# Re-ordering the passages of a feed-forward block and summing seven products in one PSUM bank

## The chip, the cores and the metric
The kernel runs on one core of a Trainium2 chip. The metric is the device time of one execution in microseconds (us). Its engines are TensorE (PE in the profile; PEld is its weight load), VectorE (DVE), ScalarE (ACT), GpSimd (POOL) and SyncE (SP), which here only issues DMAs.

## The reference
One layer of a streaming encoder on 16 meta tokens + 1024 prompt frames + 32 sample frames (T = 1072 tokens) of width 1024: RMSNorm, a combined projection for a convolution group and a windowed attention group, an output projection with residual, and then the part that the change touches:
```
def conv_ffn(x, gate_past, g, w_up, dw_w, dw_b, w_down):
    h = rmsnorm(x, g)
    u = h @ w_up                                  # 1024 -> 2 x 2816
    gate, up = u[..., :D_FF], u[..., D_FF:]
    gate_ext = jnp.concatenate([gate_past, gate], axis=1)
    y = jax.nn.silu(depthwise_causal_conv(gate_ext, dw_w, dw_b)) * up     # width 3
    return x + y @ w_down, gate_ext[:, -(FFN_CONV_WIDTH - 1):]
...
y_prompt = rmsnorm(xp, norm_final)[:, N_META:]
```
All data are float32. A float32 product is made of three matmuls in a faster float32 form: each operand is split into a high and a low part (hi, lo), and hi x hi, hi x lo and lo x hi are summed.

## The kernel before
Channels lie on the 128 partitions, tokens along the free axis. Tokens are cut into three blocks (OB and YB: 324 or 320, 384 and 352 columns) for the norms and the down-projection, and into two row blocks p = 0, 1 of 2 x 266 and 2 x 264 columns for the up-projection.

**Order.** Inside the regions of manual_schedule the instructions of TensorE run in the order in which the program writes them; in the last region (the end of the down-projection) those of ScalarE and VectorE too. Everything else, the DMA issues of SyncE among them, is put in order by the planner of the tile framework, which knows dependencies and tile releases. Each engine then runs its own list in that order.

**The second norm.** rms2(2, ...) is a generator with three steps (rms_steps, L246 to 264): sums of squares by six tiny matmuls (L252) followed by a few tiny operations on VectorE, POOL and VectorE (L253 to 257); three diagonal matrices on ScalarE (L260); six matmuls that spread the result over the partitions, R (L263), and a copy to rbg. The squares come from ScalarE and are added on POOL (L271) in conv_half before it.

**The up-projection.** There are NF = 22 feed-forward tiles f. f = 0 and 1 are plain (group: 24 matmuls of 266 or 264 columns). Meanwhile t_stage (L1216 ff.: hraw, traw, th, tl) prepares operands for the rest: f = 2 to 21 run as a seven-product scheme (Strassen's, in Winograd's form) in which seven half-size products per p take the place of eight. product makes 12 matmuls (L1205), evac reads the bank out after each product into the gate row G (two halves) and the value row Y (two halves). gate_done normalises the gate, convolves it over three taps and applies SiLU; y_done multiplies and stores y to memory (yd). w_forms prepares the seven weights of the next f, a step after every second product.

**The down-projection.** The 22 y tiles are loaded back (y_load), split, and kept in the space of operands that are no longer needed (yrow). They are consumed in three chunks; in each, eight output tiles m are made for the blocks 1, 2 and 0. d_load loads and splits a weight. In the last chunk the final norm of a block runs beside the next block's matmuls.

Of the kernel before, what the change touches and what calls it, by code (L numbers as in the profile page):

```python
# [10 lines left out]
F32 = mybir.dt.float32  # L11
F32R = mybir.dt.float32r
AF = mybir.ActivationFunctionType
ALU = mybir.AluOpType
# [3 lines left out]
P = 128  # L18
D = 1024
KD = D // P  # L20
# [74 lines left out]
CHUNKS = ((0, 6), (6, 14), (14, 22))  # L95
# [62 lines left out]
def body(nc, tc, cp, wp, xp, dp, io):  # L158
# [961 lines left out]
    with tc.tile_pool(name="psB", bufs=1, space=PSUM, reuse_waits="tile") as pf:  # L1120
# [5 lines left out]
        u2s = [xf[0][:, GOW + T:GOW + T + PNS[0]], xf[2][:, GXW + GOW:GXW + GOW + PNS[1]]]  # L1126
# [73 lines left out]
        def product(ps, q, p, f, first, last):  # L1200
# [69 lines left out]
        def evac(f, p, what, ps):  # L1270
            G, _, Y = rows_of(f)
            n, a0 = PNS[p], PAT[p]
            b0 = a0 + n
            ya, yb, u2 = Y[:, a0:a0 + n], Y[:, b0:b0 + n], u2s[p]
            add = nc.vector.tensor_tensor
            if what == 1:
                nc.scalar.copy(ya, ps)
            elif what == 6:
                add(out=u2, in0=ya, in1=ps, op=ALU.add)
            elif what == 2:  # L1280
                nc.scalar.copy(G[:, g_at(a0):g_at(a0) + n], ps)
            elif what == 7:
                add(out=yb, in0=ya, in1=ps, op=ALU.add)
            elif what == 5:
                add(out=yb, in0=yb, in1=ps, op=ALU.add)
            elif what == 4:
                add(out=ya, in0=ya, in1=ps, op=ALU.add)
            else:
                for lo_, hi_, o in g_pieces(b0, n):
                    add(out=G[:, o:o + hi_ - lo_], in0=u2[:, lo_:hi_], in1=ps[:, lo_:hi_], op=ALU.add)  # L1290

        BANK = {1: 0, 2: 0, 6: 1, 7: 1, 4: 1, 5: 2, 3: 2}
        FIRST, LAST = (1, 6, 5), (2, 4, 3)
        SEQ_ = (1, 6, 2, 7, 5, 4, 3)

        def up_strassen(f, steps):
            gate_start(f)
            banks = {}
            for q, p in steps:
                k = p, BANK[q]  # L1300
                if q in FIRST:
                    banks[k] = mmt()[:, :PNS[p]]
                product(banks[k], q, p, f, q in FIRST, q in LAST)
                evac(f, p, q, banks[k])
                yield
            gate_done(f)
            y_done(f)
# [24 lines left out]
        for i in range(4):  # L1332
            group(0, 0, i // 2, i % 2)
            next(last_rms, None)
            next(t0s)
        gate_done(0)
# [27 lines left out]
        for f in range(2, NF):  # L1364
            steps = [(q, p) for q in SEQ_ for p in range(2)]
            forms = w_forms(f + 1) if f + 1 < NF else None
            for i, _ in enumerate(up_strassen(f, steps)):
                if forms and i % 2:
                    next(forms, None)
            for _ in forms or ():  # L1370
                pass

# [8 lines left out]
        trow = [trow[i] for i in (1, 4, 2, 5, 0, 3)]  # L1381
        sr = rows(sl, 4)
        yrow = trow + list(zip(rows(BH, KD), rows(BL, KD))) + trow + [(sr[0], sr[1]), (sr[2], sr[3])]
        stage = [xf[1][:, 0:ny], xf[1][:, ny:2 * ny], gx0[:, 0:ny], rbt[:, 0:ny]]

        def y_load(f):
            raw = stage[f % 2 + 2 * (f >= CHUNKS[0][1])]
            nc.sync.dma_start(raw, yd[f][:, NMETA:T])
            hilo(*yrow[f], raw)

        bhf, blf = flat(BH), flat(BL)
        dring = [plain[:2], plain[2:]]
        big = [(z[:, i * 1024:i * 1024 + 1024], w[:, i * 1024:i * 1024 + 1024]) for i in range(6)
               for z, w in ((bhf, blf),)]
# [8 lines left out]
        def d_load(ci, m):  # L1403
            f0, f1 = CHUNKS[ci]
            w = (f1 - f0) * P
            if ci == 2 and m > 1:
                hi, lo = big[m - 2]
            else:
                hi, lo = dring[dn[0] % 2]
                dn[0] += 1  # L1410
# [14 lines left out]

        for f in range(CHUNKS[0][1]):
            y_load(f)
        wn = [d_load(0, 0)]
        order = [(ci, m) for ci in range(3) for m in range(KD)]
        for i, (ci, m) in enumerate(order[:2 * KD]):  # L1430
            w = wn.pop(0)
            wn.append(d_load(*order[i + 1]))
            for b in (1, 2, 0):
# [14 lines left out]
            if ci == 0 and m == 7:  # L1448
                y_load(20)
                y_load(21)  # L1450
# [20 lines left out]
        wz = wp.tile([P, 1024], F32, tag="raw", name="raw")  # L1471
        scrs = [z[:, i:i + 384] for z in (rbg, gx0, wz) for i in (0, 384)]
# [120 lines left out]
```

## Time and profile before
| what | value |
|---|---|
| median of 3 runs (lowest to highest) | 1106.85 us (1106.69 to 1107.34) |
| profiled execution | 1108.38 us, of which the span from the first to the last instruction is 1106.4 us |
| mean granted clock of TensorE | 0.985 of full |
| busy: TensorE, VectorE, ScalarE, POOL | 97%, 72%, 40%, 13% |

A row of a timeline begins with start and duration in us, then engine, line, operation, output<-inputs, shape and count; a bracket at its end is the idle time before it and what ended it. The up-projection begins at 353 us, the seven-product phases at about 409, the down-projection at 821, its last chunk at about 1000.

### The profile page before, as it was taken

The page shows a single profiled execution, that of the slowest core. Times are in us where ns is not written, and L with a number is a line of the kernel's source. Part 1 is how long each engine was busy: PE and PEld are TensorE (multiplying, and loading weights), DVE is VectorE, ACT ScalarE, POOL GpSimd, SP SyncE. Part 2 cuts the span into 40 slices and gives each one's busy share as a digit, 9 for nine tenths or more (in the row PEclk, how much of TensorE's full clock was granted, in tenths as well). Part 3 has the DMA queues.
Part 4 walks back from the last instruction along what each step waited for, and adds up shares of the span by engine and source line. Part 5 has one row for each costly group of instructions (what it writes and reads, how often), then busy time and mean ns, then how long its engine had stood idle before and what let it go on. Part 6 is the DMA issues. An engine that isn't in the chain of part 4 may idle for free.

```text
span 1106.4 us, 18738 instructions
## 1 busy us (share of the span) xinstructions
PE 1068.1 (97%) x7547; PEld 1039.4 (94%) x7547; DVE 799.4 (72%) x1401; ACT 437.5 (40%) x890; POOL 142.0 (13%) x189
## 2 busy tenths in 40 slices
PE   8999999989998999999999999999989999999996
PEld 7989997759998999999999999999979999999996
DVE  7789999999787888788788788788784233223233
ACT  8521227995866752233233233232244331012111
POOL 1112000013334120000000000000001210001221
PEclk9999999999999899999999999999998999999998
DMA  7344331135843111312212212212268782112012
GB/s 260 79 105 101 83 92 39 39 67 83 158 138 129 39 59 67 108 59 75 100 59 78 97 58 78 97 59 79 99 200 231 151 186 67 40 39 86 11 57 100
DMA packets 45822, 103.75 MB, mean 94 GB/s; under 512 B 7840, under 2 KB 25496, under 8 KB 45736
## 3 DMA queue, kind: packets, MB, share of 16 engines
q1 hardware_dynamic: 35912, 84.46, 23.3%
q0 software_dynamic: 9536, 17.89, 9.7%
q8 instruction: 59, 0.97, 0.4%
q14 instruction: 27, 0.22, 0.1%
q10 hardware_dynamic: 288, 0.22, 0.1%
HBM read 72.41 MB, written 21.02 MB: 84 GB/s over the span
## 4 chain that ended last, share of the span: by engine, by line
PE 83%; DVE 6%; ACT 5%; DMA 4%; issue 2%; SPq 0%; POOLq 0%; POOL 0%; DVEq 0%; ACTq 0%
PE mm L1205 36%; PE mm L240 14%; PE mm L241 14%; PE mm L242 14%; DVE acc L357 2%; DMA x<-yd 1%; DMA raw<-wdn 1%; ACT pb L688 1%; DVE tl L1137 1%; PE R L263 1%; DMA xs<-xT 1%; ACT hraw L1225 1%; ACT th L1136 1%; DVE pb L681 1%; ACT glu L750 1%
## 5 line engine op out<-in xcount | busy, mean ns | idle before, releaser
L357 DVE SCALAR_TENSOR_TENSOR acc<-glu,prm,acc 128x1090 f32<-128x1090 f32 (+3 forms) x180 | 167.9, 966 | 0.4
L1205 PE MATMUL mm<-bh,sl 128*128 128x266 f32 (+1 forms) x544 | 117.8, 285 | 0.0
L240 PE MATMUL mm<-hi,whi 128*128 128x352 f32 (+3 forms) x312 | 105.2, 337 | 2.1 <-ACT hi L274 2.1
L241 PE MATMUL mm<-lo,whi 128*128 128x352 f32 (+3 forms) x312 | 102.4, 328 | 0.5 <-DVE lo L275 0.5
L242 PE MATMUL mm<-hi,wlo 128*128 128x352 f32 (+3 forms) x312 | 102.1, 327 | 0.0
L240 PE MATMUL mm<-bh,whi 128*128 128x320 f32 (+4 forms) x320 | 99.8, 312 | 0.0
L242 PE MATMUL mm<-bh,wlo 128*128 128x320 f32 (+4 forms) x320 | 99.4, 311 | 0.0
L241 PE MATMUL mm<-bl,whi 128*128 128x320 f32 (+4 forms) x320 | 99.4, 311 | 0.0
L1205 PEld LDWEIGHTS mm<-bh,sl 128*128 128x128 f32 x544 | 90.8, 189 | 0.0
L1205 PE MATMUL mm<-th,sl 128*128 128x264 f32 (+1 forms) x384 | 90.8, 285 | 0.0
L1205 PE MATMUL mm<-bl,sl 128*128 128x266 f32 (+1 forms) x296 | 84.5, 285 | 0.0
L1205 PE MATMUL mm<-bh,whi 128*128 128x266 f32 (+1 forms) x320 | 80.8, 285 | 0.0
L1205 PEld LDWEIGHTS mm<-th,sl 128*128 128x128 f32 x384 | 66.4, 189 | 0.0
L1205 PE MATMUL mm<-th,wlo 128*128 128x266 f32 (+1 forms) x240 | 65.5, 285 | 0.0
L240 PE MATMUL mm<-th,whi 128*128 128x384 f32 (+2 forms) x180 | 59.6, 331 | 4.4 <-ACT th L1136 4.4
L240 PEld LDWEIGHTS mm<-hi,whi 128*128 128x128 f32 x312 | 59.5, 191 | 3.3 <-ACT hi L274 2.3
L240 PEld LDWEIGHTS mm<-bh,whi 128*128 128x128 f32 x320 | 61.3, 192 | 0.0
L242 PEld LDWEIGHTS mm<-bh,wlo 128*128 128x128 f32 x320 | 61.3, 192 | 0.0
L241 PEld LDWEIGHTS mm<-bl,whi 128*128 128x128 f32 x320 | 61.2, 191 | 0.0
L241 PEld LDWEIGHTS mm<-lo,whi 128*128 128x128 f32 x312 | 59.7, 191 | 1.6 <-DVE lo L275 1.2
L241 PE MATMUL mm<-tl,whi 128*128 128x384 f32 (+2 forms) x180 | 59.6, 331 | 1.5 <-DVE tl L1137 1.5
L242 PE MATMUL mm<-th,wlo 128*128 128x384 f32 (+2 forms) x180 | 59.4, 330 | 0.0
(358 smaller groups left out, 3116.2 us busy)
## 6 DMA issues: line engine op xcount, KB each, us to landing
x<-wup SPq DMA_DIRECT2D x40, 512.0 KB, 3.4
wlo<-raw POOLq DMA_DIRECT2D x16, 512.0 KB, 4.5
raw<-wdn SPq DMA_DIRECT2D x16, 512.0 KB, 3.7
raw<-win SPq DMA_DIRECT2D x14, 512.0 KB, 3.4
yd<-x SPq DMA_DIRECT2D x12, 528.0 KB, 2.7
yd<-rb SPq DMA_DIRECT2D x10, 528.0 KB, 2.7
rb<-yd SPq DMA_DIRECT2D x8, 528.0 KB, 5.1
gx<-yd SPq DMA_DIRECT2D x8, 528.0 KB, 3.7
```

The source lines that it names most:

```text
L240: nc.tensor.matmul(ps, whi(k), xhi(k), start=first and i == 0, stop=False)
L241: nc.tensor.matmul(ps, whi(k), xlo(k), start=False, stop=False)
L242: nc.tensor.matmul(ps, wlo(k), xhi(k), start=False, stop=last and i == n - 1)
L263: nc.tensor.matmul(R[:, at:at + P], ones, diag[i], start=True, stop=True)
L357: nc.vector.scalar_tensor_tensor(out=a, in0=e[:, a0 + k:a1 + k], scalar=pcol("cw", p * CW + k), in1=a, op0=ALU.mult, op1=ALU.add)
L681: last = nc.vector.tensor_tensor_reduce(out=qs_[i], in0=S, in1=bias, op0=ALU.add, op1=ALU.min, scale=1.0, scalar=3e38, accum_out=m[0][:, i ...
L688: nc.scalar.activation(qs_[i], qs_[i], AF.Exp, bias=m[0][:, i:i + 1], scale=-1.0, accum_out=m[1][:, i:i + 1])
L750: nc.scalar.copy(ptb[kv], pts[kv])
L1136: nc.scalar.copy(hi, raw)
L1137: nc.vector.tensor_tensor(out=lo, in0=raw, in1=hi.bitcast(F32), op=ALU.subtract)
L1205: nc.tensor.matmul(ps, w[:, j, :], x, start=first and j + i == 0, stop=j == 3 and i == 2, skip_group_check=True)
L1225: nc.scalar.activation(h[:, 2 * i * n + lo_:2 * i * n + hi_], src, AF.Copy, scale=pcol("g2", k))
```

## The change
1. Norm: the sums of rms2(2) move from behind the first to behind the third of the four groups of f = 0, its diagonals behind the fourth, and the R matmuls directly behind them.
2. Seven products: the order of the products is 1, 5, 6, 2, 7, 3, 4. Products 1, 6, 7 and 4 accumulate in one bank, which is read out after each (into one gate half, the other gate half, one value half, the other value half); 5 and 3 share a bank, 2 has its own. ScalarE copies after 1, 5, 6 and 4, VectorE adds after 2, 7 and 3. Except for the last f, gate_done is written behind product 3 of p = 1.
3. y loads and chunks: 8, 8 and 6 tiles in place of 6, 8 and 8. The first eight y rows are loaded inside the last f, two after products 5, 6, 7 and 3 of p = 1, through five staging buffers; the first down weight is loaded there too.
4. Last weights: two weights of the last chunk are loaded during the second chunk into free operand space, the third one ahead of the last region, the others four steps ahead; the raw buffer that served the squares is no longer taken.

```
-CHUNKS = ((0, 6), (6, 14), (14, 22))
+CHUNKS = ((0, 8), (8, 16), (16, 22))
...
-        u2s = [xf[0][:, GOW + T:GOW + T + PNS[0]], xf[2][:, GXW + GOW:GXW + GOW + PNS[1]]]
...
-            ya, yb, u2 = Y[:, a0:a0 + n], Y[:, b0:b0 + n], u2s[p]
+            ya, yb = Y[:, a0:a0 + n], Y[:, b0:b0 + n]
+            ga = G[:, g_at(a0):g_at(a0) + n]
+            gb = [(lo_, hi_, G[:, o:o + hi_ - lo_]) for lo_, hi_, o in g_pieces(b0, n)]
...
             if what == 1:
+                nc.scalar.copy(ga, ps)
+            elif what == 2:
+                add(out=ga, in0=ga, in1=ps, op=ALU.add)
+            elif what == 5:
+                nc.scalar.copy(yb, ps)
+            elif what == 6:
+                for lo_, hi_, z in gb:
+                    nc.scalar.copy(z, ps[:, lo_:hi_])
+            elif what == 7:
+                add(out=yb, in0=yb, in1=ps, op=ALU.add)
+            elif what == 3:
+                for lo_, hi_, z in gb:
+                    add(out=z, in0=z, in1=ps[:, lo_:hi_], op=ALU.add)
+            else:
                 nc.scalar.copy(ya, ps)
-            elif what == 6:
-                add(out=u2, in0=ya, in1=ps, op=ALU.add)
-            elif what == 2:
-                nc.scalar.copy(G[:, g_at(a0):g_at(a0) + n], ps)
-            elif what == 7:
-                add(out=yb, in0=ya, in1=ps, op=ALU.add)
-            elif what == 5:
-                add(out=yb, in0=yb, in1=ps, op=ALU.add)
-            elif what == 4:
-                add(out=ya, in0=ya, in1=ps, op=ALU.add)
-            else:
-                for lo_, hi_, o in g_pieces(b0, n):
-                    add(out=G[:, o:o + hi_ - lo_], in0=u2[:, lo_:hi_], in1=ps[:, lo_:hi_], op=ALU.add)
-
-        BANK = {1: 0, 2: 0, 6: 1, 7: 1, 4: 1, 5: 2, 3: 2}
-        FIRST, LAST = (1, 6, 5), (2, 4, 3)
-        SEQ_ = (1, 6, 2, 7, 5, 4, 3)
+        BANK = {1: 0, 6: 0, 7: 0, 4: 0, 5: 1, 3: 1, 2: 2}
+        SEQ_ = (1, 5, 6, 2, 7, 3, 4)
+        FIRST = (1, 5, 2)
...
                 evac(f, p, q, banks[k])
+                if (q, p) == (3, 1) and f < NF - 1:
+                    gate_done(f)
                 yield
-            gate_done(f)
+            if f == NF - 1:
+                gate_done(f)
             y_done(f)
...
             group(0, 0, i // 2, i % 2)
-            next(last_rms, None)
+            if i > 1:
+                next(last_rms)
             next(t0s)
+        next(last_rms)
         gate_done(0)
...
-        stage = [xf[1][:, 0:ny], xf[1][:, ny:2 * ny], gx0[:, 0:ny], rbt[:, 0:ny]]
+        first = [xf[1][:, 0:ny], xf[1][:, ny:2 * ny], xf[2][:, 0:ny], xf[2][:, ny:2 * ny], rbt[:, 0:ny]]
+        first += first[:3]
+        later = [gx0[:, 0:ny], rbt[:, 0:ny]]

         def y_load(f):
-            raw = stage[f % 2 + 2 * (f >= CHUNKS[0][1])]
+            raw = first[f] if f < CHUNKS[0][1] else later[f % 2]
             nc.sync.dma_start(raw, yd[f][:, NMETA:T])
             hilo(*yrow[f], raw)
...
+        AFTER = {(5, 1): (0, 1), (6, 1): (2, 3), (7, 1): (4, 5), (3, 1): (6, 7)}
+        wn = []
+        for f in range(2, NF):
+            steps = [(q, p) for q in SEQ_ for p in range(2)]
+            forms = w_forms(f + 1) if f + 1 < NF else None
+            for i, _ in enumerate(up_strassen(f, steps)):
+                if forms and i % 2:
+                    next(forms, None)
+                if forms is None and steps[i] in AFTER:
+                    for g in AFTER[steps[i]]:
+                        y_load(g)
+                    if i == 5:
+                        wn.append(d_load(0, 0))
+            for _ in forms or ():
+                pass
...
             w = wn.pop(0)
             wn.append(d_load(*order[i + 1]))
+            if ci and m > 4 and m < 7:
+                ends[m - 4] = d_load(2, m - 4)
...
-        wz = wp.tile([P, 1024], F32, tag="raw", name="raw")
-        scrs = [z[:, i:i + 384] for z in (rbg, gx0, wz) for i in (0, 384)]
+        scrs = [z[:, i:i + 384] for z in (rbg, gx0) for i in (0, 384)]
...
-        ends = dict(enumerate(wn))
+        ends[0] = wn[0]
+        ends[3] = d_load(2, 3)
         for pos, b in enumerate(EO):
             n = YB[b][1]
             for m in range(KD):
-                if not pos and m + 1 < KD:
-                    ends[m + 1] = d_load(2, m + 1)
+                if not pos and m + 4 < KD:
+                    ends[m + 4] = d_load(2, m + 4)
```

## Rows read from the trace of the kernel before

**Rows 1.** The page: busy us, share of the span, instructions.
```profile
PE 1068.1 (97%) x7547; PEld 1039.4 (94%) x7547; DVE 799.4 (72%) x1401; ACT 437.5 (40%) x890; POOL 142.0 (13%) x189
```
**Rows 2.** TensorE's waits, whole span: waiter <- releaser: us, times, longest.
```profile
PE mm L240 <- ACT th L1136: 4.4, 2, 3.9
...
PE R L252 <- POOL rb L271: 3.3, 1, 3.3
...
PE mm L242 <- DVE bl L1137: 1.9, 3, 0.6
PE mm L241 <- DVE tl L1137: 1.5, 2, 0.9
...
PE mm L240 <- ACT bh L1136: 0.9, 2, 0.5
```
**Rows 3.** TensorE's timeline in the groups of f = 0.
```profile
353.32 0.37 PE L240 MATMUL mm<-bh,whi 128*128 128x266 f32 x1
...
359.79 1.44 PE L252 MATMUL R<-ones,rb 128*128 128x1 f32 x6 [3.28 <-POOL rb L271]
361.09 0.57 PE L240 MATMUL mm<-bh,whi 128*128 128x266 f32 x1
...
366.21 0.28 PE L240 MATMUL mm<-bh,whi 128*128 128x264 f32 x1
...
370.01 1.07 PE L263 MATMUL R<-diag,ones 128*128 128x128 f32 x6 [0.74 <-ACT diag L260]
370.83 0.36 PE L240 MATMUL mm<-bh,whi 128*128 128x264 f32 x1
...
373.86 0.29 PE L240 MATMUL mm<-bh,whi 128*128 128x266 f32 x1
```
**Rows 4.** Busy time in stretches: engines' us (instructions), clock, DMA share, GB/s.
```profile
409.00:800.00 391.00, 391.00 (x3190) 391.00 (x3189) 329.46 (x509) 117.73 (x191) 25.56 (x55) 1.00 0.23 78
...
1005.00:1030.00 25.00, 22.26 (x121) 20.67 (x120) 7.72 (x10) 6.71 (x9) 5.08 (x5) 1.00 0.21 64
```
**Rows 5.** ScalarE's timeline, start of f = 20 and a y row.
```profile
781.83 1.05 ACT L1136 CAST wlo<-x 128x1024 fp32r<-128x1024 f32 x1 [3.35 <-PE mm L1205]
782.79 0.86 ACT L1277 COPY rb<-mm 128x266 f32<-128x266 f32 x2
...
812.92 1.07 ACT L1136 CAST th<-x 128x1056 fp32r<-128x1056 f32 x1 [2.76 <-DMA x<-yd]
```
**Rows 6.** TensorE's timeline at the last norm of the kernel.
```profile
1095.03 0.36 PE L252 MATMUL R<-ones,rbg 128*128 128x1 f32 x2
1097.66 1.65 PE L263 MATMUL R<-diag,ones 128*128 128x128 f32 x6 [2.28 <-ACT diag L260]
```
**Rows 7.** VectorE's timeline, first norm step and a y row.
```profile
366.50 0.15 DVE L253 TENSOR_SCALAR stat<-R 128x3 f32<-128x3 f32 x1
...
815.55 1.25 DVE L1137 TENSOR_TENSOR tl<-x,th 128x1056 fp32r<-128x1056 f32 x1
```
**Rows 8.** ScalarE's timeline in the groups of f = 0.
```profile
366.30 0.36 ACT L1325 COPY gx<-mm 128x266 f32<-128x266 f32 x1
...
369.57 0.97 ACT L260 ACTIVATE diag<-ident,stat 128x128 f32<-128x128 f32 x3
...
372.28 0.36 ACT L1325 COPY gx<-mm 128x264 f32<-128x264 f32 x1
...
375.55 1.04 ACT L1136 CAST whi<-raw 128x1024 fp32r<-128x1024 f32 x1
```
**Rows 9.** DMA issues: count, KB each, median us to landing.
```profile
x<-yd SPq DMA_DIRECT2D x6, 528.0 KB, 4.3
```
**Rows 10.** TensorE's timeline: first matmuls of the first three down slabs.
```profile
821.26 0.34 PE L240 MATMUL mm<-th,whi 128*128 128x384 f32 x1
...
839.88 0.34 PE L240 MATMUL mm<-th,whi 128*128 128x384 f32 x1
...
848.57 0.34 PE L240 MATMUL mm<-th,whi 128*128 128x384 f32 x1
```

More of the change, by code (lines that the diff above doesn't have):

```diff
@@ L1198, in moving, with product @@
             return THI[p][:, i, j, :], TLO[p][:, i, j, :]
-        def product(ps, q, p, f, first, last):
+        def product(ps, q, p, f, first):
             hi, lo = ups[f].prod[q]
@@ L1302, in up_strassen @@
                     banks[k] = mmt()[:, :PNS[p]]
-                product(banks[k], q, p, f, q in FIRST, q in LAST)
+                product(banks[k], q, p, f, q in FIRST)
                 evac(f, p, q, banks[k])
+                if (q, p) == (3, 1) and f < NF - 1:
+                    gate_done(f)
                 yield
-            gate_done(f)
+            if f == NF - 1:
+                gate_done(f)
             y_done(f)
@@ L1363, in body @@
         y_done(1)
[L1364 to L1371, printed above, removed]
         ny = T - NMETA
@@ L1380, in body @@
         trow = [(h, l) for p in range(2) for h, l in zip(rows(THI[p], 3), rows(TLO[p], 3))]
-        trow = [trow[i] for i in (1, 4, 2, 5, 0, 3)]
+        trow = [trow[i] for i in (0, 3, 1, 4, 2, 5)]
         sr = rows(sl, 4)
-        yrow = trow + list(zip(rows(BH, KD), rows(BL, KD))) + trow + [(sr[0], sr[1]), (sr[2], sr[3])]
-        stage = [xf[1][:, 0:ny], xf[1][:, ny:2 * ny], gx0[:, 0:ny], rbt[:, 0:ny]]
+        yrow = trow + [(sr[0], sr[1]), (sr[2], sr[3])] + list(zip(rows(BH, KD), rows(BL, KD))) + trow
+        first = [xf[1][:, 0:ny], xf[1][:, ny:2 * ny], xf[2][:, 0:ny], xf[2][:, ny:2 * ny], rbt[:, 0:ny]]
+        first += first[:3]
+        later = [gx0[:, 0:ny], rbt[:, 0:ny]]
         def y_load(f):
-            raw = stage[f % 2 + 2 * (f >= CHUNKS[0][1])]
+            raw = first[f] if f < CHUNKS[0][1] else later[f % 2]
             nc.sync.dma_start(raw, yd[f][:, NMETA:T])
@@ L1391, in body @@
         bhf, blf = flat(BH), flat(BL)
-        dring = [plain[:2], plain[2:]]
-        big = [(z[:, i * 1024:i * 1024 + 1024], w[:, i * 1024:i * 1024 + 1024]) for i in range(6)
-               for z, w in ((bhf, blf),)]
+        dring = [(plain[3], plain[0]), (plain[2], plain[1])]
+        slw = [sl[:, i * 1024:i * 1024 + 1024] for i in range(4)]
+        last_w = {1: slw[:2], 2: slw[2:]}
+        last_w.update({i + 3: (bhf[:, i * 1024:i * 1024 + 1024], blf[:, i * 1024:i * 1024 + 1024]) for i in range(5)})
         nscr = [0]
@@ L1405, in d_load @@
             w = (f1 - f0) * P
-            if ci == 2 and m > 1:
-                hi, lo = big[m - 2]
+            if ci == 2 and m:
+                hi, lo = last_w[m]
             else:
@@ L1424, in XY @@
             return X[b][:, m, YB[b][0] - OB[b][0]:]
-        for f in range(CHUNKS[0][1]):
-            y_load(f)
-        wn = [d_load(0, 0)]
+        AFTER = {(5, 1): (0, 1), (6, 1): (2, 3), (7, 1): (4, 5), (3, 1): (6, 7)}
[13 more added lines that the diff above has]
+                pass
+        ends = {}
         order = [(ci, m) for ci in range(3) for m in range(KD)]
@@ L1447, in body @@
                 y_load(CHUNKS[2][0] + m)
-            if ci == 0 and m == 7:
-                y_load(20)
-                y_load(21)
         region.__exit__(None, None, None)
```

## The prediction
> **What bounds the kernel now.** I read the page first, for which engine sets the end: TensorE is busy 97% of the span [rows 1], so a gain can only come from the 38 us in which it is not, or from stretches in which it runs at its lower clock. Second, the waits of TensorE [rows 2]: the reader should sort them by stage. The diff touches three of them: the norm sum and its diagonals (L252 from POOL, 3.3 us, and L263, 0.74 us, [rows 3]), the y rows at the passage out of the up-projection (L240 from ACT th, 4.4 us, and L241 from DVE tl, 1.5 us), and the last weights (bl 1.9 us and bh 0.9 us). Third, busy time by stage [rows 4]: from 409 to 800 us, where the seven-product phases run, TensorE is busy 391.00 of 391.00 us at clock 1.00. VectorE is busy 329 us there. That is much, but it ends last nowhere: relieving VectorE in this stage is worth nothing. So the seven-product stage can only lose, and the three passages can only be judged one by one.
>
> **The products in a chain of one bank.** Per row block p, VectorE did five additions and ScalarE two copies; now it is three additions and four copies. At about 0.43 us each (two copies took 0.86 us, [rows 5]) that moves some 1.7 us per f between engines that are both off the path (ScalarE is busy 118 of 391 us, [rows 4]). The matmuls stay the same in number and shape: 0. What is new is a wait. Three banks per p were reused at leisure; now bank 0 is written by 1, 6, 7 and 4 and read after each. One product is 12 matmuls of 391.00/3190 = 0.123 us, so 1.47 us. Between 1 and 6, 6 and 7, 7 and 4 of one p stand three other products, 4.4 us, against a read-out of 0.43 us, just as 1 and 2, 6 and 7, 7 and 4 stood before. But bank 0 now stays in use until product 4, second to last of f, and the next f's product 1 takes it again with one product (1.47 us) between, since six buffers go round. The copy must start within 1.0 us of its product's end. What is queued around it on ScalarE are casts of 1.05 us [rows 5]: one of them just ahead makes 0.1 + 1.05 + 0.43 = 1.6 us, 0.1 us late, two make 1.2 us. Bounds per boundary: 0 and 1.2 us; 19 boundaries: 0 to 22 us. A gain is excluded, as TensorE has no idle time to give there. I take 0, the nearer end: one cast ahead costs only 0.1 us, and two in a row ahead of a copy stand nowhere in these rows. The gate's chain on VectorE starts two products earlier in f and delays no matmul: 0.
>
> Here a rule speaks against the change. The Trainium skill, "PSUM — Partial Sum Buffer", section "PSUM bank collisions raise a hardware error", says that two engines must not touch the same bank and quadrant of partitions at the same time and that software has to fence them, so a read of a partial sum always holds up the next matmul into that bank. By the rule each of the 14 products of an f is exposed to its read-out; by the rows only the one at the boundary has less than three products of cover. By the rule at its hardest the sum would grow by up to those 22 us, by the rows by 0. No run here shows it yet; it is the rival "bank".
>
> **Passage in: the norm matmuls.** Before, the order on TensorE is group 0, sums (L252), group 1, (diagonals on ScalarE), group 2, R matmuls (L263), group 3. Group 0 begins at 353.32, the sums wait 3.28 us for POOL's last addition, and the clock falls to its lower level: group 1 takes 366.21 - 361.09 = 5.1 us where group 3 takes 373.86 - 370.83 = 3.03. From 353.32 to 373.86 is 20.5 us for work of 4 x 3.03 + 0.6 (sums) + 0.82 (R) = 13.5 us: 7.0 us are lost [rows 3]. After the change the sums stand behind group 2, at about 362.4, after POOL has delivered (359.8): the 3.28 us and the slow group go. What is late next? The chain sums, VectorE, POOL, VectorE, diagonals on ScalarE, R now has only group 3 (3.03 us) to hide in, and R stands in TensorE's queue ahead of all groups of the up weights. With nothing queued beside it this chain takes 1097.66 - 1095.39 = 2.3 us [rows 6]. In this passage it took 370.01 - 361.1 = 8.9 us, because it stood in line: the first VectorE step began only at 366.50 [rows 7]. ScalarE and VectorE are full of the seven-product operands (hraw, traw, th) here, and their order is fixed by the planner: the copy of group 0 runs at 366.30, 9.9 us after TensorE was done with it, and group 2's at 372.28 [rows 8]. That backlog belongs to ScalarE and does not shrink when TensorE gets earlier. I expect the diagonals, which now depend on group 2 and come out of the planner about when group 3 ends, where the first work after group 3 stands on ScalarE, the cast at 375.55, less the 0.97 us that the diagonals no longer take ahead of it: 374.6. R at 375.0 and the next group at 375.9, 2.0 us later than before. TensorE has then idled 9 us (group 3 ends at 366.0), and if it resumes at the lower clock, as after 3.28 us, that costs again 2.1 us on a group and 0.7 on small matmuls: 4.8 us lost in all. Bounds: the uncontended chain, 7.0 us gained; the old 8.9 us from the new sums (363.0 + 8.9 = 371.9, next group 372.7, -1.2 + 2.8), 1.6 us lost; behind the cast at 375.55 in full (R at 376.0), 5.8 us lost. I take +4.8, by the row of the copy of group 2.
>
> **Passage out: y loads and 8, 8, 6.** Six y rows were loaded after the up phase through two buffers, each waiting for the conversion before it; one load lands in 4.3 us [rows 9]. The first slab of the down-projection takes 839.88 - 821.26 = 18.6 us, the second, with the same work, 848.57 - 839.88 = 8.7 [rows 10]: 9.9 us lost, 5.9 of them idle [rows 2], the rest at the lower clock. After the change eight y rows are loaded through five buffers and converted (1.07 us on ScalarE [rows 5], 1.26 on VectorE [rows 7]) inside the last f, each pair after the product that frees its target. Room is there: in 14 x 1.47 = 20.6 us the eight casts take 8.6 and the eight subtractions 10.1, in place of the forms of a next f, which the last one does not make. The last pair waits for product 3 of p = 1, two products (2.9 us) before the end; two casts and two subtractions are then done some 3.7 us after it, 0.8 us past the end, and the first slab wants y 6 only after 18 matmuls of 384 columns, 8.7 x 384/1056 = 3.2 us. So all is hidden, with 2.4 us to spare: -9.9. Bounds: 0 if the loads stay in SyncE's line behind the store of y 20, and 9.9. More loads issue earlier on that queue, but no other load waits behind them, as no forms follow. The chunks hold the same 22 x 8 x 3 x 3 matmuls: 0.
>
> **Passage into the last chunk.** Of 25 us TensorE idles 2.7 [rows 4], in a chain of one raw buffer: load, cast, subtraction, then the next load. The other raw buffer was lent to squares; it is given back, two weights are loaded during chunk 1 and one just ahead. With 18 matmuls (3.2 us) per step instead of 24, two buffers need a load (4.3 us, as for a y row of about that size, [rows 9]) and some 2.3 us of conversion (as a y row's) per two steps of 6.3 us, with three weights ahead: about hidden. -2.7, bounds 0 and -2.7. Four square buffers instead of six still come round only after four steps: 0. The tail after the last matmul is untouched: 0.
>
> **Sum.** 4.8 - 9.9 - 2.7 = -7.8 us. The profiled execution took 1108.38 us (span 1106.40); 1100.6 on its scale. It stands 1.53 us above the median of 1106.85; on the median's scale 1099.
>
> **The rivals.**
> "Early norm": the planner lets the norm chain pass; R comes right after group 3. For it: 2.3 us uncontended is less than 3.03. Against: 8.9 us measured beside the same neighbours. 1106.85 - 7.0 - 9.9 - 2.7 = 1087. Chance 0.18.
> "Old queue": the chain keeps its 8.9 us: 1106.85 + 1.6 - 12.6 = 1096. Chance 0.14.
> "Late y": some y rows or the first weights still come after the up phase and half the passage stays: 1099 + 5 = 1104. For it: xf[2] and rb are free only when f = 20 is finished, some 7 us into the last f. Chance 0.12, two thirds of it within 0.2%.
> "Bank", the slower side: the boundary copy of product 4 sits behind work on ScalarE that is late. It decides from 7.8/19 = 0.41 us per boundary; with two casts ahead, 1.2 us, the time is 1099 + 22 = 1121. For it: a cast of 1.05 us stands ahead of the copies of product 1 at a boundary in before [rows 5]. Against: it was queued there while nothing pressed. Chance 0.16, mostly slower.
> My forecast itself has 0.40. A measurement of this kernel tells about 0.2% (2.2 us) from no change. Faster by more: 0.40 + 0.18 + 0.14 + a third of 0.12 = 0.76; within: 0.10; slower: 0.14. The range runs from the early norm, 1086, to just past late y and a mild bank wait, 1107.
>
> **What would show it.** L252's wait for POOL is gone and L263 waits near 366 to 375 us (right: about 9 us; early norm: under 1 us; then the lower clock must be absent too). No wait on th or tl and no stretch below clock 1.00 at the first slab. No bh or bl wait in the last chunk. In the seven-product stage TensorE busy 100%: any wait of its matmuls on ScalarE there is "bank", and would make the prediction wrong, as would a chain that runs past its neighbours at the first norm.

## The result, and the profile after

The changed kernel takes 1097.05 us (median of 4 runs, 1095.78 to 1097.21) beside 1106.77 for the kernel before (4 runs): ratio 0.9911, 95% interval 0.9894 to 0.9928, so 9.7 us faster. The profiled execution took 1095.78 us, span 1093.7, where that of before took 1108.38. Line numbers from the feed-forward part on differ a little from those of before (L1204 was L1205, L1330 was L1325).

The page (busy us, share, instructions) and, below it, TensorE's waits over the whole span (waiter <- releaser: us, times, longest); the waits shown are all those left of lines that the diff touches:

```profile
PE 1060.2 (97%) x7547; PEld 1033.7 (95%) x7547; DVE 775.0 (71%) x1321; ACT 468.6 (43%) x990; POOL 138.3 (13%) x189
```

```profile
PE R L263 <- ACT diag L260: 10.6, 2, 8.3
...
PE R L252 <- ACT rbg L1505: 1.0, 1, 1.0
```

Against [rows 2], the waits on POOL's rb, on th and tl, and on bh and bl are gone. In their place R waits 10.6 us for the diagonals, 2.28 of them in the tail as before [rows 6] and 8.35 in the groups of f = 0. There TensorE's timeline reads as follows, from the first group to the first product of the seven-product phases, and on to the first two slabs of the down-projection:

```profile
351.99 0.37 PE L240 MATMUL mm<-bh,whi 128*128 128x266 f32 x1
...
360.88 0.72 PE L252 MATMUL R<-ones,rb 128*128 128x1 f32 x6
361.47 0.37 PE L240 MATMUL mm<-bh,whi 128*128 128x264 f32 x1
...
372.98 1.65 PE L263 MATMUL R<-diag,ones 128*128 128x128 f32 x6 [8.35 <-ACT diag L260]
374.28 0.57 PE L240 MATMUL mm<-bh,whi 128*128 128x266 f32 x1
...
375.76 0.40 PE L240 MATMUL mm<-bh,whi 128*128 128x266 f32 x1
375.98 0.31 PE L241 MATMUL mm<-bl,whi 128*128 128x266 f32 x1
...
410.40 0.28 PE L1204 MATMUL mm<-bh,sl 128*128 128x266 f32 x1
...
822.43 0.33 PE L240 MATMUL mm<-th,wlo 128*128 128x384 f32 x1
...
834.30 0.35 PE L240 MATMUL mm<-th,whi 128*128 128x384 f32 x1
```

The sums at 360.88 wait for nothing and keep the full clock (0.72 us where they took 1.44, [rows 3]). R then stands 8.35 us idle. After it the granted clock is 0.50 (373 to 376 us), and the lower clock shows in the length of the records: a matmul of 266 columns takes 0.57 us at 374.28, 0.40 at 375.76 and 0.31 at 375.98. VectorE and ScalarE, in that stretch, show why R came at 372.98:

```profile
369.56 0.15 DVE L253 TENSOR_SCALAR stat<-R 128x3 f32<-128x3 f32 x1
```

```profile
369.89 0.36 ACT L1330 COPY gx<-mm 128x264 f32<-128x264 f32 x1
...
370.97 0.84 ACT L1135 CAST th<-traw 128x798 fp32r<-128x798 f32 x1
371.71 0.92 ACT L1224 ACTIVATE hraw<-x,prm 128x176 f32<-128x176 f32 x2
372.54 0.97 ACT L260 ACTIVATE diag<-ident,stat 128x128 f32<-128x128 f32 x3
373.42 1.03 ACT L1135 CAST whi<-raw 128x1024 fp32r<-128x1024 f32 x1
```

The sums were done at 361.60. The larger part of the delay is VectorE's line: its first norm step began 8.0 us later, behind operand steps in which VectorE and ScalarE wait for each other by turns. Its last norm step ended at 371.43, and on ScalarE the diagonals then waited 1.1 us more.

Busy time by stretch (TensorE, its weight loads, VectorE, ScalarE, POOL; then TensorE's clock, DMA share, GB/s), to be held against [rows 4]:

```profile
352.00:376.00 24.00, 15.65 (x119) 15.44 (x118) 16.93 (x35) 19.54 (x47) 4.33 (x6) 0.86 0.12 38
409.00:800.00 391.00, 391.00 (x3190) 391.00 (x3189) 307.70 (x437) 147.80 (x285) 25.63 (x55) 1.00 0.23 79
818.00:834.00 16.00, 15.98 (x108) 15.66 (x108) 14.58 (x15) 7.34 (x10) 2.95 (x3) 1.00 0.54 179
990.00:1025.00 35.00, 35.00 (x214) 35.00 (x213) 11.40 (x16) 7.14 (x11) 3.07 (x3) 1.00 0.16 45
```

The seven-product stage has as many matmuls as before in the same 391 us, while VectorE gave up 22 us of work and ScalarE took on 30. The passage out (third row) and the start of the last chunk (fourth) are full, at clock 1.00.

Put against the profiled execution of before, the 12.6 us between the two come from: passage in, first group to first product, 409.17 - 353.32 = 55.85 us before and 410.40 - 351.99 = 58.41 now, **+2.6**; seven products, from the first product to the first slab, 412.09 and 412.03 us, **0**; first down slab, 18.62 us for six y rows before [rows 10] and 834.30 - 822.43 = 11.87 for eight now. The second slab took 8.69 us before, so six rows in 18.62 lost 9.93, and eight rows, worth 8.69 x 8/6 = 11.59, lost 0.28: **-9.65**. In the last chunk, with one slab for each output tile, the last four of the first block's eight slabs took 20.9 us before, for four times 4.2 (the rows below are the first matmul of the fifth slab and the first one behind the eighth); now no slab of that block is longer than the others: **-4.1**.

```profile
1010.17 0.33 PE L240 MATMUL mm<-th,bh 128*128 128x384 f32 x1
...
1031.08 0.32 PE L240 MATMUL mm<-th,whi 128*128 128x352 f32 x1
```

The 1.3 us that the first group starts earlier lie ahead of the change; in the profiles of the runs below it starts between 350.43 and 354.56: variation from one execution to the next.

### The profile page after: what moved, and what is told of

The parts are those of the page before. It is cut to its first block, busy times and chain, and to the rows that moved or that the text cites. A ratio compares the mean times of both kernels' runs of the same rounds, so it can differ in the third digit from the quotient of the medians.

```text
span 1093.7 us, 18848 instructions
## 1 busy us (share of the span) xinstructions
PE 1060.2 (97%) x7547; PEld 1033.7 (95%) x7547; DVE 775.0 (71%) x1321; ACT 468.6 (43%) x990; POOL 138.3 (13%) x189
## 4 chain that ended last, share of the span: by engine, by line
PE 65%; ACT 2%; DVE 1%; issue 1%; POOL 0%; POOLq 0%; DVEq 0%; ACTq 0%
PE mm L1204 38%; PE mm L240 9%; PE mm L241 9%; PE mm L242 9%; ACT hraw L1224 1%; PE R L263 0%; POOL rb L271 0%; DVE x L1477 0%; ACT bh L274 0%; DVE tl L1136 0%; ACT th L1135 0%; ACT acc L270 0%; ACT diag L260 0%; DVE x L1082 0%; DVE traw L1226 0%
## 5 line engine op out<-in xcount | busy, mean ns | idle before, releaser
L1204 PE MATMUL mm<-bh,sl 128*128 128x266 f32 (+1 forms) x544 | 117.5, 285 | 0.0
L1204 PEld LDWEIGHTS mm<-bh,sl 128*128 128x128 f32 x544 | 90.7, 189 | 0.0
L1204 PE MATMUL mm<-th,sl 128*128 128x264 f32 (+1 forms) x384 | 90.2, 285 | 0.0
L1204 PE MATMUL mm<-bl,sl 128*128 128x266 f32 (+1 forms) x296 | 84.5, 285 | 0.0
L1204 PE MATMUL mm<-bh,whi 128*128 128x266 f32 (+1 forms) x320 | 80.9, 285 | 0.0
L240 PE MATMUL mm<-bh,whi 128*128 128x266 f32 (+4 forms) x224 | 68.2, 304 | 0.0
L241 PE MATMUL mm<-bl,whi 128*128 128x266 f32 (+4 forms) x224 | 67.7, 302 | 0.0
L242 PE MATMUL mm<-bh,wlo 128*128 128x266 f32 (+4 forms) x224 | 67.7, 302 | 0.0
L1204 PEld LDWEIGHTS mm<-th,sl 128*128 128x128 f32 x384 | 66.2, 188 | 0.0
L1204 PE MATMUL mm<-th,wlo 128*128 128x266 f32 (+1 forms) x240 | 65.3, 285 | 0.0
L242 PEld LDWEIGHTS mm<-hi,wlo 128*128 128x128 f32 x312 | 59.0, 189 | 0.0
L1204 PEld LDWEIGHTS mm<-bh,whi 128*128 128x128 f32 x320 | 57.1, 189 | 0.0
L1204 PEld LDWEIGHTS mm<-bl,sl 128*128 128x128 f32 x296 | 55.8, 188 | 0.0
L1204 PE MATMUL mm<-bh,wlo 128*128 128x266 f32 (+1 forms) x208 | 51.7, 284 | 0.0
L1204 PE MATMUL mm<-th,rawr 128*128 128x266 f32 (+1 forms) x208 | 49.1, 285 | 0.0
L1204 PE MATMUL mm<-bh,rawr 128*128 128x266 f32 (+1 forms) x208 | 49.0, 285 | 0.0
```

What stands on the lines that cost most here:

```text
L240: nc.tensor.matmul(ps, whi(k), xhi(k), start=first and i == 0, stop=False)
L241: nc.tensor.matmul(ps, whi(k), xlo(k), start=False, stop=False)
L242: nc.tensor.matmul(ps, wlo(k), xhi(k), start=False, stop=last and i == n - 1)
```

## Experiments

All diffs are against the changed kernel, unless the text says otherwise. Differences in us are between medians.

**1. The norm matmuls (five kernels).** norm_old puts them back:

```
 for i in range(4):
     group(0, 0, i // 2, i % 2)
-    if i > 1:
-        next(last_rms)
+    next(last_rms, None)
     next(t0s)
-next(last_rms)
```

> The changed kernel with the norm matmuls of the first feed-forward tile put back where they were (sums behind group 0, R behind group 2). Theory queue (the norm chain stands in line on ScalarE and VectorE, and TensorE loses what it waits plus the lower clock after it): the passage goes back from 9.6 us lost to 7.0 us lost, so 2.5 us faster than the changed kernel, some 12 us faster than before (1094.5 us). Rival theory operands (this stretch is bound by ScalarE and VectorE making the seven-product operands, so TensorE's waits there cost nothing): as the changed kernel within 0.5 us, 9.7 us faster than before.

Measured: 1093.71 us (1092.54 to 1094.49), ratio to before 0.9881 [0.9866, 0.9896]: 3.3 us faster than the changed kernel. The waits are those of before (3.3 us for POOL, 0.3 us for the diagonals), and the passage takes 55.90 us. The re-ordering of the norm matmuls cost time, as the prediction's term says. The other profiles agree: the passage takes 58.41 to 59.83 us, 59.12 in the mean, in the seven kernels that have the changed order of the norm and its neighbours (the changed one, bank_swap, bank_five, y_after, y_two_buffers, old_order and last_w_old), and 55.81 to 55.90 in the three with the old one (before, norm_old and chain_only), so 3.3 us by the means too. R waits 8.35 to 8.39 us in all seven. What differs is how many matmuls behind it run at the lower clock (0.42 us or more): 6 in the changed kernel, the fewest, and 21 in last_w_old.

norm_alone leaves the norm's order as changed, but holds ScalarE's and VectorE's operand work for the seven products behind the diagonals:

```
     if i > 1:
         next(last_rms)
-    next(t0s)
+behind = dlast[0].ins
+for i in range(4):
+    with tc.issue_after(behind):
+        next(t0s)
 next(last_rms)
...
-    next(t1s)
+    with tc.issue_after(behind):
+        next(t1s)
```

> The changed kernel with all operand work of the seven-product phases on ScalarE held behind the norm's diagonals; R stays behind group 3. Theory queue: with no neighbours the chain takes about 2.3 us, under the 3.0 us of group 3, so the wait of R falls from 8.35 us to under 1 us and the clock stays at full; the operands start some 10 us later, so up to 10 us of new waits stand at the start of the seven-product phases, and the time lies between 0 and 9 us under the changed kernel. Rival chain (the hops between the engines are the cost, not the line): the wait of R stays above 5 us.

Measured: 1101.51 us (1099.78 to 1101.89), ratio 0.9949 [0.9934, 0.9964], 4.5 us slower than the changed kernel. TensorE's longest waits in it:

```profile
PE mm L1204 <- ACT sl L1163: 12.5, 1, 12.5
...
PE R L263 <- ACT diag L260: 2.3, 1, 2.3
```

The 2.3 us are the tail's; the 8.35 are gone altogether. So the wait of R was its place in ScalarE's and VectorE's line and not the length of its own chain. But what was put behind came too late for the first product, at 413.29. The expectation for the time, 0 to 9 us faster, was missed: all operand work was held, and TensorE waited for it longer than it had waited for R.

norm_late lets R come three groups later, behind the third value group; norm_r1 has every step one group earlier than norm_late (counting groups from 0: sums behind group 1, diagonals behind group 2, R behind the second value group). The diff is that of norm_late:

```
-next(last_rms)
-gate_done(0)
 w_plain(1, 0, *plain[:2])
 for i in range(4):
     group(0, 1, i // 2, i % 2)
+    if i == 2:
+        next(last_rms)
+        gate_done(0)
     next(t1s)
```

> The changed kernel with the R matmuls three groups later, behind the third group of the value half of f = 0; gate_done(0) moves with them. Theory queue: the diagonals are ready at about 373 us and TensorE gets to R at about 373.5, so its wait is under 0.5 us, the clock stays at full, and the time falls by some 9 us against the changed kernel, 19 us against before (1088 us). Rival operands: the 9 us come back as waits for operands or weights at the start of the seven-product phases (about 400 us), and the time is within 2 us of the changed kernel.

> The changed kernel with the norm's matmuls spread: the sums behind gate group 1, the diagonals behind group 2 and R with its gate_done behind the second value group (the run norm_late had them one step later each, sums behind group 2, and R behind the third). Theory queue: what TensorE waits for is the work that stands ahead of the diagonals and of f=1's second weight on VectorE and ScalarE; with the diagonals and gate_done one group earlier the weight's casts also come earlier, so R waits 0 to 2 us and the wait for wlo shrinks from 5.2 us to under 3 us: 1089 to 1092 us. Rival: the same work stands in the two queues whatever the order, and what R doesn't wait the weight does: 5 to 9 us of waits in the stage, 1092 to 1096 us.

Measured: norm_late 1092.74 us (1092.3 to 1093.16), ratio 0.9873 [0.9858, 0.9888]; norm_r1 1094.12 us (1093.03 to 1094.32), ratio 0.9881 [0.9865, 0.9897]. In both, the R matmuls wait for nothing. Something else is late next, in TensorE's timeline of norm_late:

```profile
372.74 0.83 PE L263 MATMUL R<-diag,ones 128*128 128x128 f32 x6
...
384.32 0.39 PE L240 MATMUL mm<-bh,whi 128*128 128x264 f32 x1 [2.01 <-ACT whi L1135]
...
387.97 0.59 PE L242 MATMUL mm<-bh,wlo 128*128 128x264 f32 x1 [3.15 <-DVE wlo L1136]
```

f = 1's second weight now comes 5.2 us late in all (2.6 + 2.2 in norm_r1), at the lower clock (0.81 from 376 to 390), so 4.3 us are won, about half of the 9; the time lies between the two that the theory (1088) and its rival (within 2 us of the changed kernel) had named. Moving R earlier again changed these waits by 0.4 us, and the time of norm_r1 is its rival's. Was it the line again, or is there simply too much work? VectorE's timeline of norm_late just ahead of that weight's low half:

```profile
382.00 0.43 DVE L1227 TENSOR_TENSOR traw<-hraw,traw 128x264 f32<-128x264 f32 x1
382.34 1.26 DVE L1251 TENSOR_TENSOR gx<-gx,rbg 128x1060 f32<-128x1060 f32 x1
383.52 0.68 DVE L1165 TENSOR_TENSOR x<-x 128x512 f32<-128x512 f32 x1
384.12 0.69 DVE L1166 TENSOR_TENSOR x<-x 128x512 f32<-128x512 f32 x1
384.72 0.43 DVE L1229 TENSOR_TENSOR t<-hraw,traw 128x264 f32<-128x264 f32 x1
385.06 0.98 DVE L1136 TENSOR_TENSOR tl<-traw,th 128x792 fp32r<-128x792 f32 x1
385.96 0.83 DVE L1254 TENSOR_SCALAR x<-gx,prm 128x1058 f32<-128x1058 f32 x1
386.70 1.22 DVE L1136 TENSOR_TENSOR wlo<-raw,whi 128x1024 fp32r<-128x1024 f32 x1
```

Five of the seven ahead of wlo (all but the gate's 1.26 and 0.83 us) make operands of the seven products, which start at 407. held is norm_late with the last two operand steps and the first form's sums held until that weight's low half is made (diff against norm_late; w_plain now returns that step):

```
     if i == 2:
         next(last_rms)
         gate_done(0)
-    next(t1s)
+    if i < 2:
+        next(t1s)
 y_done(0)
-w_plain(1, 1, *plain[2:])
+low = w_plain(1, 1, *plain[2:])
+with tc.issue_after(low.ins):
+    next(t1s)
+    next(t1s)
...
-    if i > 3:
+    if i == 4:
+        with tc.issue_after(low.ins):
+            next(forms)
+    elif i > 4:
         next(forms)
```

> The run norm_late (1092.7 us) with two things held on VectorE and ScalarE until the low half of f=1's second weight is cast: the last two of the eight operand steps (their sums, th casts and tl subtractions), and the three sums of the first form for the seven products. In norm_late that weight made TensorE wait 2.0 us for whi and 3.2 us for wlo near 384 to 388, while the sums and subtractions ahead of wlo on VectorE (3 of 0.69, 4 of 0.43, one of 0.98) were for matmuls after 407, whose last operand there was done near 400 to 404. Theory queue order: TensorE waited for the place in line, so whi waits 0 and wlo 0 to 2 us, and nothing waits at 404 to 412: 1087 to 1090 us. Rival amount of work: VectorE and ScalarE have as much to do before the seven products start as TensorE gives them time for, and the wait comes back for sl, th or tl near 404 to 412, as it did at 413 when all eight operand steps were held behind the diagonals: 1092 to 1097 us.

Measured: 1089.86 us (1088.82 to 1090.63), ratio 0.9845 [0.9829, 0.986]: 17.2 us faster than before, 7.2 faster than the changed kernel, the best here. TensorE's only wait left between the first group and the last norm's tail:

```profile
384.49 0.59 PE L242 MATMUL mm<-bh,wlo 128*128 128x264 f32 x1 [2.89 <-DVE wlo L1136]
```

The time lies in the range of the theory, and nothing came back at 404 to 412. The remaining wait is longer than the 0 to 2 us expected, because three steps of the gate (1.26, 0.83 and 1.32 us on VectorE from 379.81) still stand ahead. So at this place too TensorE had waited for the order in line, and not for an amount of work that the two engines lack the time for. Holding back those steps alone, norm_late to held, gave 2.9 us.

**2. The chain of one bank (three kernels).** bank_swap swaps the halves of product 4, so that the bank of p = 0 is read last of all:

```
-steps = [(q, p) for q in SEQ_ for p in range(2)]
+steps = [(q, p) for q in SEQ_ for p in ((1, 0) if q == 4 else (0, 1))]
```

> The changed kernel with the two halves of product 4 in the other order (p = 1, then p = 0), so that product 1 of the next f follows right on the product whose bank it takes: no product of cover instead of one. Theory bank (a bank must be read out before TensorE writes it again, and one product of cover is what hides it now): at each of 19 boundaries TensorE waits 0.5 to 0.7 us for the copy on ScalarE, 10 to 13 us slower than the changed kernel (about 1108 us). Rival (the read-out overlaps or the boundary has slack elsewhere): within 2 us of the changed kernel.

Measured: 1096.09 us (1095.22 to 1098.83), ratio 0.9901 [0.9884, 0.9917]: as the changed kernel. No wait. TensorE at the start of an f, and ScalarE's read-out of the product 4 that ended just before:

```profile
433.62 0.28 PE L1204 MATMUL mm<-bh,whi 128*128 128x266 f32 x1
433.75 0.29 PE L1204 MATMUL mm<-bh,wlo 128*128 128x266 f32 x1
```

```profile
433.94 0.38 ACT L1292 COPY rb<-mm 128x266 f32<-128x266 f32 x1 [1.10 <-PE mm L1204]
```

The next f's product 1 runs from 433.75, ahead of the copy that reads product 4. It can't be in that bank. Buffers are handed out as they come free, and that of product 2 had long been free: no boundary is exposed. The theory fell. bank_five takes the spare cover away:

```
-return pf.tile([P, 512], F32, tag="mm", name="mm", bufs=6)
+return pf.tile([P, 512], F32, tag="mm", name="mm", bufs=5)
```

> The changed kernel with five buffers for the products in place of six. If buffers are given out as they come free, product 2 of p = 1 must take the bank of product 2 of p = 0 at once: no product of cover, 20 waits of the read-out on VectorE, 0.6 us each or more when VectorE stands at other work, 12 us or more slower than the changed kernel. Rival (a read-out never holds the next product): within 2 us.

Measured: 1112.04 us (1111.92 to 1113.43), ratio 1.0053 [1.0039, 1.0068], 15 us slower than the changed kernel. TensorE's waits, and the first on gx in its timeline:

```profile
PE mm L1204 <- DVE gx L1280: 6.4, 10, 1.7
...
PE mm L1204 <- DVE x L1280: 5.2, 10, 0.5
```

```profile
441.67 0.28 PE L1204 MATMUL mm<-bh,whi 128*128 128x266 f32 x1
442.47 0.39 PE L1204 MATMUL mm<-bh,wlo 128*128 128x264 f32 x1 [0.52 <-DVE gx L1280]
442.70 0.28 PE L1204 MATMUL mm<-bl,wlo 128*128 128x264 f32 x1
```

L1280 is the read-out of product 2. Its second half now has to take the buffer that its first half is still being read from, so each of the 20 f has one wait of a whole read-out (mostly 0.52 us). The stage grew from 412.0 to 429.0 us: 0.85 us for each, where the idle time is 0.58 in the mean. The rows show the rest: neighbours start 0.12 us apart and a record lasts 0.28, so of the 0.80 us from 441.67 to 442.47 some 0.68 are lost and 0.52 count as idle; and the next matmul starts 0.23 us later, not 0.12. That is 0.27 us beside the idle time, 5.4 in 20 waits, and 17.0 - 11.6 is 5.4.

chain_only is the kernel before with the new order, chain and place of gate_done, and nothing else:

```
-BANK = {1: 0, 2: 0, 6: 1, 7: 1, 4: 1, 5: 2, 3: 2}
-SEQ_ = (1, 6, 2, 7, 5, 4, 3)
+BANK = {1: 0, 6: 0, 7: 0, 4: 0, 5: 1, 3: 1, 2: 2}
+SEQ_ = (1, 5, 6, 2, 7, 3, 4)
...
+if (q, p) == (3, 1) and f < NF - 1:
+    gate_done(f)
```

> The kernel before with only the new order of the seven products, their chain in one bank and the earlier gate_done. Theory (TensorE sets the pace of this stage and no read-out holds it): the time of before within 2 us, no wait of TensorE between 409 and 800 us. Rival relief (two additions fewer per row block on VectorE shorten the stage): over 2 us faster. Rival bank (read-outs hold the next product): over 2 us slower, with waits of TensorE on ScalarE or VectorE in the stage.

Measured: 1102.72 us (9 runs, 1100.57 to 1106.57), ratio 0.9967 [0.9954, 0.998]: 3.8 us faster than before, where neither theory has room for a gain. The seven-product stage is as long as ever; it is the first down slab that is shorter, 12.55 us after 18.62 (in the profiled execution, the fastest of the nine, 7.8 us below that of before; what spreads the nine is open). ScalarE's casts of y rows, before and in chain_only:

```profile
814.15 1.08 ACT L1136 CAST th<-x 128x1056 fp32r<-128x1056 f32 x1 [0.16 <-PE mm L1205]
...
828.16 1.07 ACT L1136 CAST th<-x 128x1056 fp32r<-128x1056 f32 x1 [1.46 <-DMA x<-yd]
```

```profile
807.05 1.08 ACT L1136 CAST th<-x 128x1056 fp32r<-128x1056 f32 x1
...
809.08 1.09 ACT L1136 CAST th<-x 128x1056 fp32r<-128x1056 f32 x1
...
822.32 1.07 ACT L1136 CAST th<-x 128x1056 fp32r<-128x1056 f32 x1 [0.69 <-DMA x<-yd]
```

The y rows are cast into the operands of products 5, 6 and 7, which now stand at places 2, 3 and 5 of an f and not 5, 2 and 4. Product 7's come free later, but product 5's earlier, and these count: the first two rows fill both load buffers, and before, one of them could be cast only at 814.15, when product 5 of p = 0 ended (its row lies in product 6's part but, in rows of 1056 columns cut from parts of 1064, starts in the last eight columns of product 5's). Now both are cast by 810.17, and the last of the six casts starts at 822.32, where it started at 828.16 before. Before, each of the six subtractions on VectorE began within 0.4 us of the end of its cast, so fewer additions there are not the cause. This is a gain of the new order, at the passage out; whether another choice of target rows would have given it in the old order was not run.

**3. The passage out (three more kernels).** y_after writes the eight loads and the first down weight behind the last f and leaves all else:

```
-if forms is None and steps[i] in AFTER:
-    for g in AFTER[steps[i]]:
-        y_load(g)
-    if i == 5:
-        wn.append(d_load(0, 0))
...
+for g in range(CHUNKS[0][1]):
+    y_load(g)
+wn.append(d_load(0, 0))
```

> The changed kernel with the eight y loads and the first down weight written behind the last f instead of inside it; five staging buffers and chunks of 8, 8 and 6 as changed. Theory place (the loads were late because they were written behind the up phase): most of the 9.6 us of the passage comes back, 6 to 10 us slower than the changed kernel. Rival buffers (five staging buffers are what matters, the planner finds the place by itself): within 2 us of the changed kernel.

y_two_buffers gives the eight loads two buffers and not five; old_order has the products' old order and sums, with each pair of loads behind the product whose operand it takes (behind 6, 7, 5 and 3). old_order's first down weights overwrite slots that its product 5 still reads, so it leaves out that product's right values in the last f, with the same work.

```
-first += first[:3]
+first = [first[i % 2] for i in range(8)]
```

```
-SEQ_ = (1, 5, 6, 2, 7, 3, 4)
+SEQ_ = (1, 6, 2, 7, 5, 4, 3)
...
-AFTER = {(5, 1): (0, 1), (6, 1): (2, 3), (7, 1): (4, 5), (3, 1): (6, 7)}
+AFTER = {(6, 1): (0, 1), (7, 1): (2, 3), (5, 1): (4, 5), (3, 1): (6, 7)}
```

> The changed kernel with one edit: the eight first y rows go through two load buffers by turns and not five (three of them used twice). Theory buffers: most of the 9.7 us won at the passage out came from having more buffers; each load then waits for both casts of the row two before it, and waits for y rows come back at the first slab of the down product: 3 to 9 us slower than the changed kernel, with TensorE waits on th, tl, bh or bl near 822. Rival targets: what counts is that the rows that receive the casts come free earlier in the last gate product; a load took 4.3 us in the kernel before and its row is free some 3 us apart from the next, so two buffers give no more than one late row: within 2 us of the changed kernel, no wait over 1 us near 822.

> The changed kernel with the seven products in the order and with the sums of the kernel before (1, 6, 2, 7, 5, 4, 3 in three banks), its gate_done back at the end, and the y loads written behind the products 6, 7, 5 and 3 of the second part, whose rows they take. Theory order: the earlier position of products 5, 6 and 7 is what let the y rows in; on the kernel before the new order alone gave 3.8 us, so 3 to 5 us slower than the changed kernel, with a wait on th or tl near 822. Rival buffers: five buffers make up for the later targets, and the y rows are in place when the first slab starts: within 1.5 us of the changed kernel, no wait over 1 us near 822.

Measured, with the length of the first slab and what it is above the second slab's rate (8.69 us for six rows, 11.59 for eight):

| kernel | us, median (lowest to highest) | ratio to before | first slab, us | lost, us |
|---|---|---|---|---|
| before | 1106.77 | | 18.62, six rows | 9.9 |
| chain_only | 1102.72 (1100.57 to 1106.57) | 0.9967 [0.9954, 0.998] | 12.55, six rows | 3.9 |
| changed | 1097.05 (1095.78 to 1097.21) | 0.9911 [0.9894, 0.9928] | 11.87, eight rows | 0.3 |
| y_after | 1096.67 (1095.91 to 1096.96) | 0.991 [0.9897, 0.9922] | 11.87, eight rows | 0.3 |
| y_two_buffers | 1107.58 (1106.91 to 1111.07) | 1.0012 [1.0002, 1.0022] | 23.96, eight rows | 12.4 |
| old_order | 1103.09 (1101.52 to 1106.4) | 0.9961 [0.9947, 0.9975] | 18.41, eight rows | 6.8 |

TensorE's timeline of y_two_buffers and of old_order at that slab:

```profile
829.47 0.44 PE L241 MATMUL mm<-tl,wlo 128*128 128x384 f32 x1 [4.07 <-DVE tl L1136]
...
834.92 0.69 PE L240 MATMUL mm<-sl,wlo 128*128 128x384 f32 x1 [3.28 <-ACT sl L1135]
```

```profile
830.51 0.45 PE L240 MATMUL mm<-th,wlo 128*128 128x384 f32 x1 [2.09 <-ACT th L1136]
832.58 0.69 PE L241 MATMUL mm<-tl,wlo 128*128 128x384 f32 x1 [1.62 <-DVE tl L1137]
```

Where the loads are written does nothing: in y_after the casts still run from 807.75 to 821.72, inside the last f, so the planner moves them up as buffers and rows come free. With two buffers the whole gain is lost, and 6.0 of 9.7 us with the old order: eight rows need both. (The slab of old_order is that of its slowest run, so its 6.8 us stand beside 6.0 between medians.) The two expectations that named a size were short of what came (3 to 9 us, 10.5 measured; 3 to 5, 6.0 measured).

**4. The last weights.** last_w_old loads them as before:

```
-if ci and m > 4 and m < 7:
-    ends[m - 4] = d_load(2, m - 4)
...
+wz = wp.tile([P, 1024], F32, tag="raw", name="raw")
...
-if not pos and m + 4 < KD:
-    ends[m + 4] = d_load(2, m + 4)
+if not pos and m + 1 < KD:
+    ends[m + 1] = d_load(2, m + 1)
```

> The changed kernel with the last weights as before: no early loads, one step ahead, one raw buffer lent to the squares. Theory: the chain of one raw buffer sets the pace of the first slabs again. By the idle time read in before it costs 2.7 us against the changed kernel; by the lengths of the slabs (20.9 us for four that need 16.8) 4.1 us; with slabs of 18 instead of 24 matmuls the chain is less covered, so up to 8 us. Rival: hidden, within 1 us.

Measured: 1101.91 us (1100.63 to 1102.79), ratio 0.9957 [0.9945, 0.9968]: 4.9 us slower than the changed kernel, with the waits of before on bh and bl (3.7 us in six):

```profile
PE mm L240 <- ACT bh L1135: 2.6, 3, 1.0
...
PE mm L242 <- DVE bl L1136: 1.1, 3, 0.4
```

## Why the prediction was right, and where it was not

It gave 1099 us and came out 2 us high: the mechanism of each passage was right, with two terms mis-sized, and one step of the argument was wrong without moving the sum.

**Passage in, +4.8; measured +2.6 in the profile, +3.3 by norm_old.** R was to wait about 9 us with the diagonals just ahead of the cast of the next weight; it waited 8.35, with the diagonals at 372.54 and the cast at 373.42. From the first group to the one behind R it took 22.29 us, where 22.6 was worked out and 20.54 taken before. The mis-sized term is the clock: 2.8 us, taken from the group after POOL's wait. Here only R and six or seven matmuls ran at the lower level, and of the 2.6 us 0.8 are left for it; in the other six profiles with this order 1.2 to 2.2 are, so the profiled execution is the mildest, and the size of the term was in part chance. That the cause is the line was shown by norm_alone; but the prediction gave the backlog to ScalarE, and 8.0 us of it passed before VectorE's first step. The rival "old queue" had 1096 us, nearer to the 1097.05 than the forecast, so the time alone does not tell them apart. The chain does: from the sums' end to R it took 11.4 us, where the forecast had 12.0 and that rival 8.9.

**Passage out, -9.9; measured -9.65.** All was hidden, as worked out, but not by the place that the loads have in the program: y_after writes them behind the last f and loses nothing. What counts is the number of buffers (y_two_buffers) and the places of products 5, 6 and 7 (old_order, chain_only). The prediction gave the new order 0 and held that "a gain is excluded, as TensorE has no idle time to give there". That is the step that failed: it looked for the gain in the stage that was edited, and the gain lay where that stage's operand rows are used next. The sum didn't suffer only because the passage out had been given the whole of its loss as a gain already, and a loss can be won back only once.

**The chain of one bank, 0; measured 0** (412.09 and 412.03 us). The reason given was wrong. "Six buffers go round" was an assumption; bank_swap shows that a freed buffer is taken out of turn, so there was no boundary with one product of cover. The rival "bank" had no place to occur. The rule weighed there holds: the Trainium skill, "PSUM — Partial Sum Buffer", section "PSUM bank collisions raise a hardware error", has the read-out held apart from the next write to the bank. The trace of bank_five, which leaves no cover at one product of each f, agrees: the write waits 0.52 us there for the read-out, at 0.85 us each. With six buffers the trace shows no such wait.

**Last chunk, -2.7; measured -4.1 in the profile, -4.9 by last_w_old** (whose slabs are shorter and hide less). Right in kind. The term took TensorE's idle time in 25 us [rows 4]; but there are five short waits in it [rows 2], and each costs some 0.27 us beside its idle time, as in bank_five: 2.7 + 1.4 = 4.1.

**Sum.** 2.6 - 9.65 + 0 - 4.1 = -11.2 and the 1.3 us ahead of the change make the -12.6 between the two profiled executions, within rounding; between medians it is -9.7, since that of before was 1.6 us above its median and that of after 1.3 below.

## What to carry to other kernels

When a matmul is moved, don't only ask whether its operand could be ready: look at where in the line of the slower engines the planner puts the work that makes it, and hold back there what is needed later, but no more than that. In this passage the later place of the R matmuls gave 4.3 us and made another operand late; holding two operand steps and one weight's sums behind that operand gave 2.9 more (held); holding all the operand work cost 4.5 (norm_alone). When the order of a stage changes, look for gains and losses in the next stage that re-uses its operand rows, and count both buffers and free targets, since either alone gave back most of the gain. And size a wait from the length of the stretch, not from the idle time alone.

## What the runs showed of the hardware

- A wait costs more than its idle time even at clock 1.00: in bank_five 20 waits of 11.6 us in all lengthened the stage by 17.0 us. The records overlap (0.28 us long, 0.12 apart), so about 0.16 us of a stop are not counted as idle, and the first matmul behind it took 0.39 us where its neighbours took 0.28.
- The lower clock after a longer idle time need not last longer, nor the same after the same one. After waits of 3.25 to 3.31 us (before, norm_old, chain_only) it held for about 3.3 to 6.7 us; after waits of 8.35 to 8.39 us, in seven profiles, for about 2.8 to 6.1 us. How much of it a wait brings has to be read at that wait, and in more than one execution.
